# Output projection by block products: which weight parts are prepared in the attention, by which engine, and which in the stage itself

## The chip, the cores and the metric

One core of one Trainium2 chip runs the whole kernel. The metric is the device time of one execution in microseconds. Five engines work side by side, each in its own order of instructions: TensorE (PE in the profile; PEld is its weight load), VectorE (DVE), ScalarE (ACT), GpSimd (POOL) and SyncE (SP, which issues most DMAs).

## The reference

A decoder trunk of two layers, T = 1024 tokens, width D = 1024, all in fp32. Cut to the output projection and what stands on either side of it:

```python
merged = g_a * (o_a @ w_br[l, :OUT_A]) + g_b * (o_b @ w_br[l, OUT_A:])
x = x + merged @ w_o[l]                  # (1024, 1024) @ (1024, 1024)
h2 = rmsnorm(x, norm2[l])
up = h2 @ w_up[l]                        # then a ConvFFN, w_up is (1024, 5632)
```

Ahead of it stand an RMSNorm, one input projection, a dilated window attention (o_a) and a stick-breaking attention (o_b). g_a and g_b are sigmoids of gate columns of the input projection.

## The kernel before, in words

**Products.** Each fp32 operand x is kept as two parts in a reduced type, hi = round(x) and lo = x − hi; a product is three matmuls, hi·hi, hi·lo and lo·hi (`product`, L185). The parts come from `split` (L145): ACT casts hi (L148), DVE subtracts to lo (L156). Weights are loaded raw by SP into the tag "wr" (NRAW = 2 buffers) and split from there (`weights`, L164).

**The output projection** `merged @ w_o` takes w_o and the merged activations as 2 × 2 blocks and forms seven block products (k = 0 to 6) instead of eight, of sums and differences of blocks. Each product is four e-blocks of 128 output columns, and each e-block 12 matmuls: four i, three matmuls each. The order is 0, 4, 1, 2, 3, 5, 6 (`out_proj`, L1379). Four of the seven weight operands are sums or differences of blocks of w_o. After an e-block DVE adds the result to the residual x (L1455), and `norm_add` (L481) squares x on ACT (L487) and adds to a running sum of squares on DVE (L489). Sums for half 0 of x are done by k = 3, and PE takes them with a small product, nrm_t (L544), ahead of the second norm. Half 1 follows at the end of the stage.

**The weight operands are prepared ahead**, in the attention. `prepare` (L1328) is a generator: the scheduler of dense work (`share`, L312) asks it for one step per unit of dense work from the 15th on (PREP = 14). It takes four blocks of w_br and eight of w_o. A block is loaded into the tag "ot", which has one buffer (w_one); three steps later its parts follow, one a step. Each part, w_two, is an ACT copy (L1337), a DVE subtraction (L1338) and a DMA (L1339) to DRAM: `brd` for the branch weights, `wod` for the seven operands. Block sums are formed in place on DVE (L1342). That is 4 × 7 + 8 × 10 = 108 steps in a layer.

**The attention around it.** PE interleaves dense pairs of the input projection with attention items. The last pair is a values' pair (`pair_v`, L1294). For each of its quarters PE transposes into v_t (L1300), ACT and DVE make vv (L1305, L1306), and a DMA sends it off (L1311); vv too lives in "ot". Stick-breaking items (`stick_item`, L712) have scores z, a gate beta on ACT (L729), a diagonal select on GpSimd (L735), a scan and a product on DVE (L749, L756), transposes sb_t on PE, and outputs sb_o (L668) that DVE gathers in ob (L678).

**The branch stage** (in `mixer`, L1462) multiplies the two attention outputs by w_br (br_ps, L190 to L192), two outputs of columns to one loaded block br_w (`branch_in`, L1562), weighs with the gates (gin, L1620, L1625), merges, and forms sums c11, c12, c21 for the projection.

**The up projection.** `up_plain` (L1777) starts the first ffn unit: up_weights(0, 0) and (0, 1) are loaded and split (w_raw, w_hi, w_lo) when it starts, right behind the last block product; PE's u_ps (L190 to L192) uses them, and then takes nrm_t of half 1.

PE's instruction order comes from these generators. The scheduler places what ACT, DVE, GpSimd and SP do by priority; each engine then works strictly through its list.

Of the kernel before, what the change touches and what calls it, by code (L numbers as in the profile page):

```python
# [16 lines left out]
P = 128  # L17
# [48 lines left out]
def trunk_kernel(ctx, tc, x, norm1, w_in, b_gate, w_br, w_o, norm2, w_up, conv_w, conv_b, w_down, norm_f, out, depth=None, probe=None):  # L66
# [54 lines left out]
    wod = dr.tile([7, 4, P, 2, 512], F32, name="wod")  # L121
    brd = dr.tile([4, P, 2, T], F32, name="brd")
# [1205 lines left out]
    def prepare(l):  # L1328


        many = 0

        def out(src, there):
            nonlocal many
            t = small("w_two", F32R) if many % 2 else sb.tile([P, 512], F32R, tag="bias", name="w_two")
            many += 1
            act.copy(t[:, 0:256], src)  # L1337
            yields(dve.tensor_tensor(t[:, 256:512], src, f32(t[:, 0:256]), ALU.subtract))  # L1338
            nc.sync.dma_start(there, f32(t).rearrange("p (h n) -> p h n", h=2))  # L1339

        def into(dst, a, b, op):
            yields(dve.tensor_tensor(dst, a, b, op))  # L1342

        def load(src):
            raw = sb.tile([P, 4, 256], F32, tag="ot", name="w_one")
            nc.sync.dma_start(raw, src)
            return [raw[:, i, :] for i in range(4)]

        for e2 in range(4):
            blocks = load(w_br[l].rearrange("(k p) n -> p k n", p=P)[:, :, 256 * e2 : 256 * e2 + 256])  # L1350
            for _ in range(3):
                yield
            for k, x in enumerate(blocks):
                out(x, brd[e2][:, :, 256 * k : 256 * k + 256])
                yield
        for i in range(4):
            for c in range(2):
                raw = sb.tile([P, 2, 2, 256], F32, tag="ot", name="w_one")
                for j in range(2):
# [3 lines left out]
                for _ in range(3):  # L1363
                    yield
                col = slice(256 * c, 256 * c + 256)
                for k, x in ((0, a11), (3, a22), (4, a12)):
                    out(x, wod[k, i][:, :, col])
                    yield
                for k, dst, x, y, op in (
                    (2, a11, a11, a21, ALU.subtract),  # L1370
                    (5, a21, a21, a22, ALU.add),
                    (1, a22, a22, a11, ALU.subtract),
                    (6, a12, a12, a22, ALU.subtract),
                ):
                    into(dst, x, y, op)
                    out(dst, wod[k, i][:, :, col])
                    yield

    def out_proj(keep):  # L1379
# [7 lines left out]
        def load(at):  # L1387
            if at >= len(order):
                return
            k = order[at]  # L1390
            ws[k] = []
            for i in range(4):
                if at % 2 == 0:
                    if i % 2 == 0:
                        t = sb.tile([P, 2, 2, 512], F32R, tag="ql", bufs=2, name="wo_in")
                    nc.sync.dma_start(f32(t[:, i % 2]), wod[k, i])
                    ws[k].append((t[:, i % 2, 0, :], t[:, i % 2, 1, :]))
                else:
                    w = [sb.tile([P, 512], F32R, tag=tag, bufs=4, name="wo_in") for tag in ("wh", "wl")]
                    for h in range(2):  # L1400
                        nc.sync.dma_start(f32(w[h]), wod[k, i][:, h, :])
                    ws[k].append(w)
# [9 lines left out]

        def beside(k, e):
            c11, c12, c21 = keep[0, 0], keep[1, 0], keep[0, 1]
            if k == 0:
# [3 lines left out]
                split(*sums[1][e], c11[:, e, :])  # L1419
            elif k == 4:  # L1420
                dve.tensor_tensor(c21[:, e, :], c21[:, e, :], c11[:, e, :], ALU.subtract)
                if e == 0:
                    new_sum(2)
                split(*sums[2][e], c12[:, e, :])
                if e == 3:
                    x_in(1, 0)
            elif k == 1:
                if e == 0:
                    new_sum(3)
                split(*sums[3][e], c21[:, e, :])  # L1430
                if e == 3:
                    x_in(1, 1)
                    x_in(0, 1)

        load(0)
        load(1)
        yield
        for at, k in enumerate(order):
# [4 lines left out]
            for e in range(4):  # L1443
# [13 lines left out]
                if k > 2:  # L1457
                    norm_add(n, 4 * f + e, e == 0 and k in (4, 5), acc[:, n, :])
                yield
            load(at + 2)  # L1460

    def mixer(l, pending):  # L1462
# [140 lines left out]
        for i, ab in order:  # L1603
# [28 lines left out]
            if i == 9:  # L1632
                wo = out_proj(keep)
                next(wo)
# [16 lines left out]
    def ffn(l, pending, final):  # L1651
# [125 lines left out]
        def up_plain(j, order, turns, extra):  # L1777
# [3 lines left out]
            w = [up_weights(j, 0), up_weights(j, 1)]  # L1781
# [597 lines left out]
```

## Time and profile before

| | |
|---|---|
| median of 3 runs | 2703.09 us (2701.85 to 2704.11) |
| the profiled execution | 2700.12 us, span 2698.4 us, mean granted TensorE clock 0.984 |
| busy, share of the span | PE 96%, PEld 80%, DVE 80%, ACT 50%, POOL 4% |
| POOL | 111.4 us in 137 instructions |

How to read it: busy times are sums over one execution. A row of a timeline gives the start, the length, engine, line, operation, output <- inputs, and in brackets how long the engine had been idle and what ended that. `x4` is the number of equal instructions in a row. A releaser such as `DVE ob L678` is the last thing waited for by the profile. PEclk, or the column after the engines in a table of stretches, is the TensorE clock granted in that stretch, 1.00 being full. A matmul of 128 × 512 follows the one before by 0.23 us at full clock.

### The profile page before, as it was taken

Reading aid. Unit: us, or ns where it says so; the run is one execution under the profiler, and the core shown is the slowest. Engines: PE = TensorE matmul, PEld = TensorE weight load, DVE = VectorE, ACT = ScalarE, POOL = GpSimd, SP = SyncE. Lnnn points to the kernel's source line nnn. Section 1 sums busy time; section 2 is a strip of 40 time slices with the busy share of each in tenths; the row PEclk is TensorE's granted clock in tenths of the full one; section 3 lists DMA queues with packets and bytes.
Section 4 is the critical chain, followed back from the end, with each engine's and each line's share of the span. In section 5 each row is a group of like instructions: output and inputs, shape, how many; then the busy total and the mean of one; then the engine's idle time right before and its main releaser. Section 6 shows DMA issues by size and latency. Waiting matters only on the chain. (4 is left out here: it accounts for less than half of the span.)

```text
span 2698.4 us, 36486 instructions
## 1 busy us (share of the span) xinstructions
PE 2602.4 (96%) x12551; PEld 2164.6 (80%) x12551; DVE 2150.6 (80%) x3701; ACT 1361.9 (50%) x2609; POOL 111.4 (4%) x137
## 2 busy tenths in 40 slices
PE   9997899999899999999999978999998999999999
PEld 8876688887788888888887757888787888888887
DVE  8887777786788888897678878777858888888965
ACT  6555566663455555522445545665624545454224
POOL 3000000011000000000000020000200000000000
PEclk9998999999999999999999989999999999999999
DMA  7665667985234444588347656879752343546963
GB/s 251 217 225 189 203 192 211 253 280 217 76 130 159 152 145 159 210 334 319 142 154 230 220 173 201 220 203 259 271 203 71 136 158 137 172 141 247 340 249 127
DMA packets 428165, 537.75 MB, mean 199 GB/s; under 512 B 27700, under 2 KB 331468, under 8 KB 425164
## 3 DMA queue, kind: packets, MB, share of 16 engines
q1 hardware_dynamic: 427116, 533.02, 60.0%
q0 software_dynamic: 704, 2.13, 0.3%
q8 instruction: 99, 1.62, 0.2%
q14 instruction: 86, 0.70, 0.1%
q10 hardware_dynamic: 160, 0.27, 0.0%
HBM read 334.95 MB, written 200.38 MB: 198 GB/s over the span
## 5 line engine op out<-in xcount | busy, mean ns | idle before, releaser
L148 ACT CAST w_hi<-up_a 128x512 fp32r<-128x512 f32 x280 | 174.1, 623 | 277.3 <-DVE up_a L1827 120.3
L156 DVE TENSOR_TENSOR w_lo<-up_a,w_hi 128x512 fp32r<-128x512 f32 x280 | 189.4, 688 | 83.8 <-ACT w_hi L148 83.8
L148 ACT CAST w_hi<-in_a 128x512 fp32r<-128x512 f32 x252 | 155.9, 623 | 130.5 <-DVE in_a L1195 31.7
L156 DVE TENSOR_TENSOR w_lo<-in_a,w_hi 128x512 fp32r<-128x512 f32 x252 | 172.1, 686 | 60.3 <-ACT w_hi L148 57.2
L1984 DVE TENSOR_TENSOR x<-x,d_ps 128x512 f32<-128x512 f32 x220 | 150.2, 684 | 60.0 <-PE d_ps L1975 56.7
L1064 PE MATMUL u_a<-hh,w_hi 128*128 128x512 f32 x320 | 124.5, 389 | 0.0
L1065 PE MATMUL u_a<-hl,w_hi 128*128 128x512 f32 x320 | 124.5, 389 | 0.0
L1066 PE MATMUL u_a<-hh,w_lo 128*128 128x512 f32 x320 | 124.5, 389 | 0.0
L1064 PE MATMUL u_a<-t_hi,w_hi 128*128 128x512 f32 x320 | 124.5, 389 | 0.0
L1065 PE MATMUL u_a<-t_lo,w_hi 128*128 128x512 f32 x320 | 124.5, 389 | 0.0
L1066 PE MATMUL u_a<-t_hi,w_lo 128*128 128x512 f32 x320 | 124.5, 389 | 0.0
L1973 PE MATMUL d_ps<-gd_in,w_hi 128*128 128x512 f32 x316 | 123.2, 390 | 0.0
L1974 PE MATMUL d_ps<-gd_in,w_hi 128*128 128x512 f32 x316 | 123.0, 389 | 0.0
L1975 PE MATMUL d_ps<-gd_in,w_lo 128*128 128x512 f32 x316 | 122.9, 389 | 0.0
L1064 PE MATMUL i_a<-hh,w_hi 128*128 128x512 f32 x288 | 119.6, 415 | 0.1
L1064 PE MATMUL i_a<-t_hi,w_hi 128*128 128x512 f32 x288 | 117.2, 407 | 1.8 <-ACT u L1212 1.8
L1066 PE MATMUL i_a<-hh,w_lo 128*128 128x512 f32 x288 | 114.6, 398 | 0.0
L1065 PE MATMUL i_a<-hl,w_hi 128*128 128x512 f32 x288 | 114.0, 396 | 0.0
L1337 ACT CAST w_two<-w_one 128x256 fp32r<-128x256 f32 x144 | 57.5, 410 | 111.0 <-DVE w_one L1342 43.8
L1066 PE MATMUL i_a<-t_hi,w_lo 128*128 128x512 f32 x288 | 113.2, 393 | 0.0
L1065 PE MATMUL i_a<-t_lo,w_hi 128*128 128x512 f32 x288 | 113.1, 393 | 0.0
L1973 PE MATMUL d_ps<-gd_in,wd 128*128 128x512 f32 x284 | 111.0, 391 | 0.0
(423 smaller groups left out, 7895.2 us busy)
## 6 DMA issues: line engine op xcount, KB each, us to landing
gd<-g SPq DMA_DIRECT2D x154, 512.0 KB, 3.2
gd_in<-gd SPq DMA_DIRECT2D x154, 512.0 KB, 6.5
up_a<-in_w_up_dram SPq DMA_DIRECT2D x80, 512.0 KB, 5.1
in_a<-in_w_in_dram SPq DMA_DIRECT2D x72, 512.0 KB, 5.9
wod<-w_two SPq DMA_DIRECT2D x112, 256.0 KB, 2.5
wd_raw<-in_w_down_dram SPq DMA_DIRECT2D x22, 1024.0 KB, 13.1
wo_in<-wod SPq DMA_DIRECT2D x32, 512.0 KB, 4.9
gin<-gs SPq DMA_DIRECT2D x32, 512.0 KB, 4.8
```

The costliest lines, as they stand in the source:

```text
L148: one = act.copy(hi, src)
L156: two = dve.tensor_tensor(lo, src, f32(hi), ALU.subtract)
L1064: pe.matmul(o, w[0][:, c], rh, start=(first and i == 0), stop=False, skip_group_check=True)
L1065: pe.matmul(o, w[0][:, c], rl, start=False, stop=False, skip_group_check=True)
L1066: pe.matmul(o, w[1][:, c], rh, start=False, stop=(last and i == 3), skip_group_check=True)
L1337: act.copy(t[:, 0:256], src)
L1973: pe.matmul(o, wh[:, c], gh, start=(i == 0 and k in (0, 4, 5)), stop=False, skip_group_check=True)
L1974: pe.matmul(o, wh[:, c], gl, start=False, stop=False, skip_group_check=True)
L1975: pe.matmul(o, wl[:, c], gh, start=False, stop=(i == m - 1), skip_group_check=True)
L1984: dve.tensor_tensor(x, x, o, ALU.add)
```

## The change

`prepare` no longer makes parts of w_br, and takes seven steps for a w_o block, 56 in a layer. It makes the parts of k = 0, 4, 2 and 1 alone, with the subtraction on GpSimd; the block sums too move to GpSimd, and the two of k = 5 and 6 go to DRAM unsplit (`wof`). So a layer has 32 ACT copies here instead of 72, 64 GpSimd operations, and none on DVE.

`out_proj` loads k = 0, 4, 1 and 2 ready, in halves; k = 3 raw from w_o, k = 5 and 6 raw from `wof`, through "wr" (`load_raw`), and splits them on ACT and DVE in the stage (`two`). Squares of x are added one product earlier or later by a rule of their own (`square`), and the residual half x_in(1, 1) is fetched earlier. The first up weights are loaded and split beside k = 5 (`early["up"]`). `branch_in` loads raw w_br (half the bytes) through "wr" and splits it.

```diff
 def out(src, there):
     act.copy(t[:, 0:256], src)
-    yields(dve.tensor_tensor(t[:, 256:512], src, f32(t[:, 0:256]), ALU.subtract))
+    pool.tensor_tensor(t[:, 256:512], src, f32(t[:, 0:256]), ALU.subtract)
     nc.sync.dma_start(there, f32(t).rearrange("p (h n) -> p h n", h=2))
...
-for e2 in range(4):
-    blocks = load(w_br[l].rearrange("(k p) n -> p k n", p=P)[:, :, 256 * e2 : 256 * e2 + 256])
-    for _ in range(3):
-        yield
-    for k, x in enumerate(blocks):
-        out(x, brd[e2][:, :, 256 * k : 256 * k + 256])
-        yield
...
-for k, x in ((0, a11), (3, a22), (4, a12)):
-    out(x, wod[k, i][:, :, col])
-    yield
-for k, dst, x, y, op in (
-    (2, a11, a11, a21, ALU.subtract),
-    (5, a21, a21, a22, ALU.add),
-    (1, a22, a22, a11, ALU.subtract),
-    (6, a12, a12, a22, ALU.subtract),
-):
-    into(dst, x, y, op)
-    out(dst, wod[k, i][:, :, col])
-    yield
+out(a11, wod[0, i][:, :, col])
+yield
+out(a12, wod[4, i][:, :, col])
+pool.tensor_tensor(a11, a11, a21, ALU.subtract)
+yield
+out(a11, wod[2, i][:, :, col])
+pool.tensor_tensor(a21, a21, a22, ALU.add)
+nc.sync.dma_start(wof[0, i][:, col], a21)
+yield
+pool.tensor_tensor(a22, a22, a11, ALU.subtract)
+out(a22, wod[1, i][:, :, col])
+pool.tensor_tensor(a12, a12, a22, ALU.subtract)
+nc.sync.dma_start(wof[1, i][:, col], a12)
+yield
...
+def load_raw(k):
+    raws[k] = []
+    for i in range(0, 4, 2):
+        t = sb.tile([P, 2, 512], F32, tag="wr", bufs=NRAW, name="wo_raw")
...
+        nc.sync.dma_start(t, src)
+        raws[k] += [t[:, 0, :], t[:, 1, :]]
+def two(k, *some):
...
+    for i in some:
+        split(*ws[k][i], raws[k][i])
...
+elif k == 2:
+    square(0, 0, e, True)
+    if e in (1, 2):
+        two(3, 2 * e - 2, 2 * e - 1)
+    if e == 2:
+        load_raw(5)
+elif k == 3:
+    square(0, 1, e, False)
+    if e < 2:
+        two(5, 2 * e, 2 * e + 1)
+    if e == 1:
+        load_raw(6)
+    if e == 3:
+        two(6, 0, 1, 2, 3)
+elif k == 5:
+    square(1, 1, e, True)
+    if e == 0:
+        early["up"] = []
+    if e < 2:
+        early["up"].append(weights(w_up[l][:, e * DFF : e * DFF + P], P))
+else:
+    square(1, 0, e, False)
...
 e, wb = todo[i][1], big("br_w", F32R)
-nc.sync.dma_start(f32(wb), brd[e // 2])
+raw = sb.tile([P, 4, 256], F32, tag="wr", bufs=NRAW, name="br_raw")
+nc.sync.dma_start(raw, w_br[l].rearrange("(k p) n -> p k n", p=P)[:, :, e * P : (e + 2) * P])
+for q in (1, 0):
+    split(*parts_[q], raw[:, 2 * q : 2 * q + 2, :])
...
-w = [up_weights(j, 0), up_weights(j, 1)]
+w = early.pop('up') if j == 0 else [up_weights(j, 0), up_weights(j, 1)]
```

**What it moves.** PE's order is the same before and after. At three places the order of other engines differs; the numbers in a name only tell one buffer's use from another.

The first place is ACT at the last values' pair of the attention, layer 0. Before, parts of a w_o block (w_two) and the splits of dense inputs (in_a) and scores (sb_t) come ahead of three vv in a row:

```order
L1337 CAST w_two_2908<-w_one_2770 128x256
L1337 CAST w_two_2923<-w_one_2770 128x256
L148 CAST sbh_2932<-sb_t_2927 128x512
L148 CAST w_hi_2937<-in_a_2592 128x512
L1337 CAST w_two_2957<-w_one_2770 128x256
L1337 CAST w_two_2973<-w_one_2770 128x256
L1305 CAST vv_2809<-v_t_2804 128x4x2x64
L1305 CAST vv_2873<-v_t_2868 128x4x2x64
L1305 CAST vv_2952<-v_t_2947 128x4x2x64
L148 CAST w_hi_2988<-in_a_2592 128x512
```

After, at the same place:

```order
L1305 CAST vv_2759<-v_t_2754 128x4x2x64
L148 CAST sbh_2774<-sb_t_2770 128x384
L677 COPY fold_2796<-sb_o_2648 64x256
L148 CAST w_hi_2781<-in_a_2577 128x512
L1251 COPY last_2808<-i_a_2587 128x512
L1305 CAST vv_2815<-v_t_2810 128x4x2x64
L729 ACTIVATE beta_2819<-z_2820 128x512
L730 ACTIVATE stay_2735<-z_2820 128x512
L148 CAST w_hi_2831<-in_a_2577 128x512
L1212 COPY u_2835<-i_a_2838 128x512
```

No w_two is left there; the first vv stands ahead of `last`, and each of the next is further along, with work of the pair between them.

The second place is GpSimd in the stick-breaking items of layer 0. Before, it does selects only:

```order
L689 MEMSET slots_898 64x4x256
L735 AFFINE_SELECT beta_1019<-beta_1019 128x128
L735 AFFINE_SELECT beta_1044<-beta_1044 128x128
L735 AFFINE_SELECT beta_1075<-beta_1075 128x128
L735 AFFINE_SELECT beta_1160<-beta_1160 128x128
L735 AFFINE_SELECT beta_1310<-beta_1310 128x128
```

After, from the same clearing of `slots` on (L1338 makes a part, L1355 to L1363 form the block sums):

```order
L689 MEMSET slots_898 64x4x256
L1338 TENSOR_TENSOR w_two_1240<-w_one_1193,w_two_1240 128x256
L1355 TENSOR_TENSOR w_one_1193<-w_one_1193 128x256
L1358 TENSOR_TENSOR w_one_1193<-w_one_1193 128x256
L1361 TENSOR_TENSOR w_one_1193<-w_one_1193 128x256
L735 AFFINE_SELECT beta_1019<-beta_1019 128x128
L735 AFFINE_SELECT beta_1044<-beta_1044 128x128
L1338 TENSOR_TENSOR w_two_1284<-w_one_1193,w_two_1284 128x256
L735 AFFINE_SELECT beta_1075<-beta_1075 128x128
L735 AFFINE_SELECT beta_1160<-beta_1160 128x128
L1338 TENSOR_TENSOR w_two_1259<-w_one_1193,w_two_1259 128x256
```

The same selects, 1019, 1044 and 1075, stand behind and between parts and block sums of the first w_o block.

The third place is DVE at the end of the output stage, layer 0. Before, the up weights' parts w_lo come after the last sum of squares (L489):

```order
L156 TENSOR_TENSOR t_lo_7237<-s3_7252,t_hi_7236 128x512
L156 TENSOR_TENSOR t_lo_7237<-s3_7262,t_hi_7236 128x512
L489 TENSOR_TENSOR nrm_6560<-nrm_6560,sq_7273 128x512
L156 TENSOR_TENSOR t_lo_7237<-s3_7276,t_hi_7236 128x512
L489 TENSOR_TENSOR nrm_6560<-nrm_6560,sq_7293 128x512
L156 TENSOR_TENSOR w_lo_7299<-w_raw_7296,w_hi_7298 128x512
L156 TENSOR_TENSOR w_lo_7305<-w_raw_7302,w_hi_7304 128x512
L156 TENSOR_TENSOR w_lo_7311<-w_raw_7308,w_hi_7310 128x512
L156 TENSOR_TENSOR w_lo_7317<-w_raw_7314,w_hi_7316 128x512
L547 RECIPROCAL ss_7334<-ss_7334 128x4
```

After, they stand at product k = 3, between the adds to x0 (L1490, before L1455) and the sums of squares of half 0:

```order
L489 TENSOR_TENSOR nrm_6428<-nrm_6428,sq_6920 128x512
L156 TENSOR_TENSOR w_lo_7016<-w_raw_7013,w_hi_7015 128x512
L1490 TENSOR_TENSOR x0_6829<-x0_6829,o_ps_6594 128x512
L156 TENSOR_TENSOR w_lo_7022<-w_raw_7019,w_hi_7021 128x512
L489 TENSOR_TENSOR nrm_6428<-nrm_6428,sq_6942 128x512
L1490 TENSOR_TENSOR x0_6829<-x0_6829,o_ps_6595 128x512
L156 TENSOR_TENSOR w_lo_7052<-w_raw_7049,w_hi_7051 128x512
L489 TENSOR_TENSOR nrm_6428<-nrm_6428,sq_6966 128x512
L156 TENSOR_TENSOR w_lo_7058<-w_raw_7055,w_hi_7057 128x512
L1490 TENSOR_TENSOR x0_6829<-x0_6829,o_ps_6596 128x512
L489 TENSOR_TENSOR nrm_6428<-nrm_6428,sq_6982 128x512
```

And the end of the stage now reads:

```order
L156 TENSOR_TENSOR t_lo_7151<-s3_7166,t_hi_7150 128x512
L156 TENSOR_TENSOR t_lo_7151<-s3_7176,t_hi_7150 128x512
L489 TENSOR_TENSOR nrm_6428<-nrm_6428,sq_7187 128x512
L156 TENSOR_TENSOR t_lo_7151<-s3_7190,t_hi_7150 128x512
L489 TENSOR_TENSOR nrm_6428<-nrm_6428,sq_7207 128x512
L547 RECIPROCAL ss_7224<-ss_7224 128x4
```

The four w_lo have moved from behind the last sum of half 1 to ahead of the last sum of half 0; the order of what ends the stage is otherwise the same.

More of the change, by code (lines that the diff above doesn't have):

```diff
@@ L120, in trunk_kernel @@
     gd = dr.tile([NF // 2, 7, P, 2, HF], F32, name="gd")
-    wod = dr.tile([7, 4, P, 2, 512], F32, name="wod")
-    brd = dr.tile([4, P, 2, T], F32, name="brd")
+    wod = dr.tile([5, 4, P, 2, 512], F32, name="wod")
+    wof = dr.tile([2, 4, P, 512], F32, name="wof")
     obd = dr.tile([P, 2, T], F32, name="obd")
@@ L1411, in part, with square @@
             return h_part(int(k > 4), 2 * i + int(k in (4, 6)))
+        def square(n, f, e, first):
+            norm_add(n, 4 * f + e, first and e == 0, acc[:, n, :])
         def beside(k, e):
@@ L1419, in beside @@
                 split(*sums[1][e], c11[:, e, :])
+                if e == 3:
+                    load(1)
             elif k == 4:
-                dve.tensor_tensor(c21[:, e, :], c21[:, e, :], c11[:, e, :], ALU.subtract)
                 if e == 0:
```

58 lines of the change are left out of this document (29 added, 29 removed).

## The prediction

> **What bounds the kernel now.** I read the engines' shares first, then the list of what TensorE waits for, then a table of the stretches in which its clock was low, and last the rows around each long wait. The first part of the page:
>
> ```profile
> PE 2602.4 (96%) x12551; PEld 2164.6 (80%) x12551; DVE 2150.6 (80%) x3701; ACT 1361.9 (50%) x2609; POOL 111.4 (4%) x137
> ```
>
> TensorE is the bound: 2602 us of a span of 2698.4. The change leaves its matmuls and their order as they are, so it can only win what TensorE loses in waits, and in the slow clock behind them. The list of waits, TensorE only, both layers together (total, times, longest):
>
> ```profile
> PE u_ps L192 <- DVE w_lo L156: 15.1, 2, 7.5
> PE v_t L1300 <- DVE vv L1306: 13.2, 2, 6.7
> PE v_t L1300 <- DVE ob L678: 9.7, 2, 5.1
> PE br_ps L190 <- DMA br_w<-brd: 9.0, 3, 4.3
> PE sb_o L668 <- DVE ob L678: 8.5, 2, 4.5
> PE sb_o L668 <- DVE vv L1306: 6.7, 2, 3.3
> ```
>
> Three families stand out. Four rows (v_t and sb_o) belong to the last values' pair of the attention, 250 to 310 us in layer 0 and 1585 to 1645 in layer 1: 13.2 + 9.7 + 8.5 + 6.7 = 38.1 us. One (br_w) is the branch products' weights, 9.0 us. One (u_ps) is the first up product behind the output projection, 15.1 us. Each is followed by a stretch at half clock. The table of stretches (length, TensorE's busy time and matmuls, weight loads, DVE, ACT, POOL, then the granted clock):
>
> ```profile
> 252.47:259.30 6.83, 4.73 (x13) 3.89 (x14) 5.48 (x11) 4.05 (x9) 0.56 (x1) 0.50 0.30 94
> 266.13:276.37 10.24, 4.11 (x14) 3.25 (x15) 2.33 (x5) 1.70 (x4) 0.00 (x0) 0.50 0.46 166
> 303.67:307.09 3.42, 2.90 (x9) 2.48 (x10) 2.51 (x5) 0.37 (x1) 0.00 (x0) 0.50 0.85 268
> 610.87:617.70 6.83, 4.81 (x11) 3.80 (x12) 6.66 (x10) 4.62 (x9) 2.57 (x2) 0.50 0.78 244
> 706.45:716.68 10.23, 4.87 (x13) 3.91 (x14) 6.33 (x11) 3.30 (x6) 0.00 (x0) 0.50 0.18 53
> 1587.08:1590.50 3.42, 3.39 (x10) 2.90 (x11) 3.16 (x6) 2.33 (x5) 0.56 (x1) 0.50 0.36 115
> 1597.32:1610.98 13.66, 6.52 (x21) 5.25 (x22) 4.37 (x9) 4.05 (x8) 0.00 (x0) 0.50 0.40 144
> 1638.28:1641.70 3.42, 3.42 (x10) 2.65 (x9) 1.55 (x3) 1.62 (x4) 0.29 (x1) 0.50 0.63 217
> ```
>
> At clock 0.50 half of the busy time is loss. For the values' pair that is (4.73 + 4.11 + 2.90 + 3.39 + 6.52 + 3.42) / 2 = 12.5 us, so the whole family costs 38.1 + 12.5 = **50.6 us**. The br_w family costs 9.0 + 4.81 (half of it, in two layers) = 13.8, the u_ps family 15.1 + 4.87 = 20.0. All three: 84.4.
>
> **The values' pair: +50.6.** Timeline rows of TensorE and ACT there, in layer 0, then two groups with their durations (least, median, most, in ns) and the start of their first and last:
>
> ```profile
> 254.57 1.12 PE L1300 MATMUL v_t<-ident,u 128*128 128x128 f32 x4 [5.14 <-DVE ob L678]
> 268.92 1.11 PE L1300 MATMUL v_t<-ident,u 128*128 128x128 f32 x4 [6.44 <-DVE vv L1306]
> ```
> ```profile
> 252.82 0.40 ACT L1337 CAST w_two<-w_one 128x256 fp32r<-128x256 f32 x1 [4.11 <-DMA w_one<-in_w_o_dram]
> ```
> ```profile
> 266.65 0.40 ACT L1337 CAST w_two<-w_one 128x256 fp32r<-128x256 f32 x1 [0.40 <-DMA wod<-w_two]
> 267.55 0.59 ACT L1305 CAST vv<-v_t 128x512 fp32r<-128x512 f32 x1 [0.49 <-DVE w_two L1338]
> 271.92 0.59 ACT L1305 CAST vv<-v_t 128x512 fp32r<-128x512 f32 x1 [3.79 <-DMA sv<-vv]
> ```
> ```profile
> L1300 PE MATMUL v_t<-ident,u x72: 270/272/476, 243.9 to 1770.1; 128*128 128x128 f32 x72
> ```
> ```profile
> L1337 ACT CAST w_two<-w_one x144: 399/407/467, 76.9 to 1662.2; 128x256 fp32r<-128x256 f32 x144
> ```
>
> ACT stands 4.11 us at a weight part whose load has not landed. DVE's subtraction of that part stands behind it, and ob (L678), which needs nothing of the weights, is queued next on DVE; TensorE waits for ob until 254.57. Then vv and w_one take turns in the one buffer "ot". All parts of the block come first, the last at 266.65, and three vv come in a row from 267.55, 4.4 us apart because each waits for the DMA of the one before. TensorE meets them at 268.92 (6.44) and once more. The wait near 304 is again ob behind a part.
>
> In the changed order there are 56 steps of preparation instead of 108, paced by the same clock. The part at 266.65 is step 88 (28 steps of branch parts, six blocks of 10), the first at 76.9 is step 4: 189.75 / 84 = 2.26 us a step. 56 steps end near 76.9 + 52 × 2.26 = 194, ahead of the pair's first v_t at 243.9. No w_one is left in "ot" then, each vv follows its v_t, and ob has no part ahead of it. What is late next? The two v_t rows lie 14.35 us apart; without the 6.44 and half of the 4.73 it is 5.5, more than the 4.4 that one vv takes. So the chain keeps up by a microsecond, and I leave nothing of the wait.
>
> **The preparation on GpSimd: −4 (−20 to +10).** The nearest rows for what is taken away and what it is put on:
>
> ```profile
> L1338 DVE TENSOR_TENSOR w_two<-w_one,w_two 128x256 fp32r<-128x256 f32 x144 | 59.2, 418 | 49.2 <-ACT w_two L1337 46.5 <-DMA slots<-sq 1.2 <-DMA obd<-ob 0.5
> ```
> ```profile
> L735 POOL TENSOR_SCALAR_AFFINE_SELECT beta<-beta 128x128 f32<-128x128 f32 x64 | 44.7, 700 | 593.8 <-ACT beta L729 530.6 <-DVE w_lo L156 30.9 <-DVE w_one L1342 25.2
> L1585 POOL TENSOR_TENSOR hl<-m_part,hh 128x512 fp32r<-128x512 f32 x16 | 24.7, 1550 | 161.2 <-ACT hh L1584 161.2
> L2270 POOL TENSOR_TENSOR h_raw<-hh,hl 128x256 f32<-128x256 f32 x8 | 7.1, 914 | 0.0
> ```
>
> Per layer DVE loses 72 parts of 0.42 us and 32 block sums of the same shape (43.5 us), ACT 40 of its 72 parts of 0.41; GpSimd gains 64. No row has this shape as a subtraction on GpSimd beside a busy DVE. From below 0.91 us (L2270, same size, nothing beside it), from above 1.55 (L1585, twice the size, DVE full). I take 0.95, nearest to the row of the same size: 64 × 0.95 = 61 us in some 120. That fits, so the preparation does end before the pair. The price is that the 15 or so diagonal selects per layer (L735), now run at once, stand behind up to five or six parts in GpSimd's queue; behind the select stand DVE's L756 on the same scores and TensorE's transposes. TensorE has other work there, so most of it is hidden; I take 2 us a layer. Ends: 10 lost a layer (every select 0.7 us late on the path), or 5 gained (DVE freed of what it did for the preparation until 194: half of the 43.5).
>
> The Trainium skill, "GPSIMD Engine Reference", section 3.1, speaks against this part: two-input elementwise work takes twice as long there as on VectorE, so VectorE should keep it. The rows agree on the ratio (0.914 to 0.42 us); by the rule the step would lose, but GpSimd is 4% busy here and DVE 80%, and I side with those shares; what is left of the rule is rival D.
>
> **The branch stage: 0 (−8 to +8).** brd is gone, raw branch weights are split in the stage. Rows of TensorE and of DVE, the second from just ahead of TensorE's wait:
>
> ```profile
> 612.89 0.77 PE L190 MATMUL br_ps<-oh_a,br_w 128*128 128x512 f32 x1 [4.34 <-DMA br_w<-brd]
> ```
> ```profile
> 607.88 0.68 DVE L1620 TENSOR_TENSOR gin<-gin,br_ps 128x512 f32<-128x512 f32 x1
> ```
>
> The wait named is the DMA's, from 608.5 to 612.89. But by the program's order this L1620 takes the 20th product, and TensorE has finished 24: DVE is four behind and works on without a gap until 625. The changed order has one more DVE operation up to the last gate (four splits of br_w in, three c21 and one m_lo out: 64 for 63). Removing the DMA's wait moves the wait to DVE, and TensorE's 4.3 us stay under another name. Ends: the DMA wait goes (+4 a layer), or a second split late behind the gates costs as much.
>
> **The output stage: −6 (−20 to 0).** The k = 3, 5 and 6 weights come raw, through the two "wr" buffers, then the up weights through the same two.
>
> ```profile
> 682.16 0.69 DVE L489 TENSOR_TENSOR nrm<-nrm,sq 128x512 f32<-128x512 f32 x1 [0.76 <-ACT sq L487]
> ```
> ```profile
> 683.24 0.95 PE L544 MATMUL nrm_t<-ones,nrm 128*128 128x1 f32 x8
> ```
> ```profile
> wo_in<-wod SPq DMA_DIRECT2D x32, 512.0 KB, 4.9
> ```
>
> The first half's sum of squares is done at 682.85 and TensorE takes it at 683.24 with no slack. In the changed order this last add on DVE stands behind the fourth up split. One block of a product is 12 matmuls of 0.22 us (0.44 at half clock, from the rows of the next part), a product four blocks, 10.6 us. The row at 683.24 stands one block behind the end of k = 3, so k = 3 begins near 683.2 − 2.6 − 10.6 = 670; raw6 is asked for at its second block, about 674, lands 4.9 later at 679, is split by 681, and only then is its buffer free for the second up part: landed at 684 to 686, cast, split and add 2 us more. I take 3 us late a layer, from 0 (the loads overlap better) to 7, or 10 with the clock. That the clock falls after a short wait is seen here:
>
> ```profile
> 179.30 0.50 PE L1064 MATMUL i_c<-hh,w_hi 128*128 128x512 f32 x1 [2.19 <-ACT u L1217]
> ```
> ```profile
> 180.79:184.21 3.42, 3.42 (x12) 2.83 (x11) 3.13 (x6) 1.89 (x5) 0.42 (x1) 0.50 0.50 130
> ```
>
> After 2.19 us of idling came 3.42 us at half clock, 1.7 us lost. The Trainium skill, "TensorE: Matmul & The Clock Gate", section "HAM oscillation", has as its rule that gaps over about 3.4 us are the ones to avoid. By that rule a new 3 us wait would cost no clock, and this part's low end would be −14; this trace says that it may, and it decides.
>
> **The first up product: +6 (4 to 10), not 20.** Rows at the end of the stage:
>
> ```profile
> 710.47 0.68 DVE L489 TENSOR_TENSOR nrm<-nrm,sq 128x512 f32<-128x512 f32 x1
> 711.07 1.28 DVE L156 TENSOR_TENSOR w_lo<-w_raw,w_hi 128x512 fp32r<-128x512 f32 x2
> ```
> ```profile
> 703.87 0.39 PE L191 MATMUL u_ps<-hl,w_hi 128*128 128x512 f32 x1
> 711.81 0.80 PE L192 MATMUL u_ps<-hh,w_lo 128*128 128x512 f32 x1 [7.55 <-DVE w_lo L156]
> ```
> ```profile
> 716.24 1.16 PE L544 MATMUL nrm_t<-ones,nrm 128*128 128x1 f32 x8
> ```
>
> From 711.81 TensorE does 10 matmuls in 4.43 us at half clock, 0.44 each. With w_lo early it does them right behind the one at 703.87, at 0.22 each, until 706.3, and then needs the second half's sum of squares. DVE ends that at 711.15, and its queue up to there is the same and without gaps. So a wait of 4.7 takes the place of 7.55: nrm_t comes 5 us sooner, less 2 us of half clock that then falls on later matmuls. 3 a layer.
>
> **Sum.** 50.6 − 4 + 0 − 6 + 6 = 46.6. The profiled execution took 2700.12 (1.7 around its span), 2.97 less than the median: 2700.1 − 46.6 + 3.0 = **2656**.
>
> **Rivals.** (B) All three families go: −84, **2619**. For it: each has its cause removed by name. Against: the add at 710.47, and DVE four products behind at 607.88. (C) The stage's new chain through "wr" is slow, TensorE waits 10 us or more a layer at nrm_t with the clock halved, and something of the values' pair stays: half the gain, **2678**. (D, slower) The selects behind the parts on GpSimd hold DVE and then TensorE. With 30 selects it eats all 46.6 from 1.6 us each on; at 3 us each, which six parts in a row at L1585's 1.55 would give (up to 9 us for one), it is 2703.1 + 90 − 46.6 = **2746**. Against it: parts of 0.9 us, and TensorE's spare work. (E) The change doesn't do what it says: at over 2.9 us a part (64 × 2.9 = 186 us) GpSimd is still preparing at 260, the vv wait in "ot" as now, and it comes out near **2702**.
>
> **Numbers.** A measurement here tells about 0.2% (5.4 us) from no change. Forecast 0.63, C 0.19, B 0.09, D 0.06, E 0.03. Faster 0.91, same 0.03, slower 0.06. The range takes in the forecast's own spread (all terms at a bad end don't come together) and C to 2688; at the other end it takes 26 us more than forecast, 2630. B, D and E are left out, 0.18.
>
> **What would show it.** Right: no w_two on ACT after about 200 us; v_t and sb_o gone from TensorE's waits; full clock from 250 to 310; a br_ps wait on DVE or gates; nrm_t waiting on nrm (L489) in place of u_ps on w_lo. Wrong: waits of sb_t or z that rise before 215 (D); parts on GpSimd well over 1 us; a wait of nrm_t near 683 over 5 us (C); no wait near 706 (B).

## The result, and the profile after

The changed kernel took 2670.71 us (median of 4 runs, 2669.2 to 2671.88), the kernel before beside it 2702.47. The ratio is 0.9882, with a 95% interval of 0.9865 to 0.9899: faster by 31.8 us, where 46.6 had been forecast. Its profiled execution took 2670.32 us, its span is 2668.6.

The engines' shares in the changed kernel:

```profile
PE 2597.4 (97%) x12551; PEld 2163.0 (81%) x12551; DVE 2137.4 (80%) x3533; ACT 1358.8 (51%) x2569; POOL 226.0 (8%) x265
```

TensorE is where it was; GpSimd has doubled, from 111.4 to 226.0 us. The list of TensorE's waits, after (total, times, longest):

```profile
PE i_a L1064 <- DVE u L1242: 13.1, 4, 5.5
PE nrm_t L544 <- DVE nrm L489: 12.3, 5, 4.8
PE i_b L1064 <- DVE u L1228: 10.2, 6, 2.3
PE br_ps L192 <- DVE br_w L156: 5.1, 3, 2.2
PE z L654 <- ACT stay L730: 4.6, 6, 2.6
PE i_c L1064 <- ACT u L1217: 4.3, 2, 2.2
PE i_c L1064 <- ACT last L1251: 3.7, 4, 1.3
```

All four rows of the values' pair are gone, as is u_ps on w_lo; nrm_t on nrm stands in its place, as forecast. Two more rows are new, i_a and i_b on u, 23.3 us together. They belong to the dense pairs of the attention, and their places say where. The same two stretches of layer 0, first of the kernel before, then of the changed one (length, busy time and instructions of PE, PEld, DVE, ACT, POOL, then the granted clock and the DMA columns):

```profile
76.00:216.00 140.00, 133.43 (x654) 108.67 (x652) 114.94 (x207) 78.32 (x177) 6.73 (x16) 0.99 0.68 220
216.00:340.00 124.00, 100.27 (x466) 80.50 (x467) 97.37 (x180) 67.18 (x148) 7.96 (x13) 0.90 0.58 190
```
```profile
76.00:216.00 140.00, 117.56 (x557) 93.86 (x556) 102.98 (x137) 67.97 (x152) 67.69 (x79) 0.97 0.61 199
216.00:340.00 124.00, 123.53 (x629) 102.53 (x628) 100.30 (x160) 70.08 (x142) 10.61 (x17) 0.99 0.44 143
```

After 216 us TensorE is now busy nearly without a break, 123.5 of 124 us at clock 0.99. But from 76 to 216, where it had been nearly as full (133.4 of 140), it is down to 117.6. That is the stretch in which GpSimd works 67.7 us.

TensorE's instructions have the same order in both kernels, so their starts can be set side by side, one by one. In layer 0 the changed kernel is 0.96 us ahead near 27 us and 21.1 behind at 204 (times of before): **22.0 lost**. It is 13.1 ahead at 355: **34.1 won**. In layer 1 it loses 21.7 and wins 34.2. The branch stage wins 2.6 and 4.3; from the first block product into the up projection it is 0.9 slower in layer 0 and 1.1 faster in layer 1. Together 68.3 − 43.7 + 6.9 + 0.2 = 31.7. That this is nearly the gain of the medians, 31.8, is chance: the two executions set side by side differ by 29.8 in span. Beside the terms of the sum stand 1.0 us won ahead of 27 us and 2.3 lost between the attentions and the branch stages (1.6 and 0.8).

So what is to be explained above all is one number: 22 us a layer lost before 205 us, where the prediction had 2. Rows of the largest wait there (ACT, DVE and TensorE of the changed kernel):

```profile
206.31 0.41 ACT L1337 CAST w_two<-w_one 128x256 fp32r<-128x256 f32 x1 [7.46 <-DMA w_one<-in_w_o_dram]
206.62 0.58 ACT L148 CAST sbh<-sb_t 128x512 fp32r<-128x512 f32 x1
```
```profile
207.29 0.69 DVE L156 TENSOR_TENSOR sbl<-sb_t,sbh 128x512 fp32r<-128x512 f32 x1 [5.51 <-ACT sbh L148]
207.90 0.98 DVE L1192 TENSOR_TENSOR in_a<-in_a 128x512 f32<-128x512 f32 x1
210.97 1.23 DVE L156 TENSOR_TENSOR w_lo<-in_a,w_hi 128x512 fp32r<-128x512 f32 x1 [2.10 <-ACT w_hi L148]
212.12 0.67 DVE L1242 TENSOR_TENSOR u<-u,i_b 128x512 f32<-128x512 f32 x1
```
```profile
212.94 0.77 PE L1064 MATMUL i_a<-hh,w_hi 128*128 128x512 f32 x1 [5.51 <-DVE u L1242]
```

They offer two readings. ACT stands 7.46 us at a part whose block has not landed, with the cast sbh behind it, DVE behind that, and TensorE at the end: the stall of the values' pair over again, in another place. Or one looks at the lengths: w_lo takes 1.23 us in place of 0.68, L1192 takes 0.98.

**Theory 1, the one buffer**: the reload of w_one waits for GpSimd's last block sum and for the DMA that sends the sum off, and ACT waits for the reload. **Theory 2, GpSimd beside DVE**: GpSimd's work makes DVE's operations longer, and DVE is what TensorE waits for here.

### The profile page after: what moved, and what is told of

Read it like the earlier page. It is cut to its first block, busy times and chain, and to the rows that moved or that the text cites. A ratio compares the mean times of both kernels' runs of the same rounds, so it can differ in the third digit from the quotient of the medians.

```text
span 2668.6 us, 36222 instructions
## 1 busy us (share of the span) xinstructions
PE 2597.4 (97%) x12551; PEld 2163.0 (81%) x12551; DVE 2137.4 (80%) x3533; ACT 1358.8 (51%) x2569; POOL 226.0 (8%) x265
## 4 chain that ended last, share of the span: by engine, by line
PE 67%; DVE 4%; DMA 3%; ACT 2%; issue 1%; POOL 1%; SPq 1%; DVEq 0%; POOLq 0%; ACTq 0%
PE u_a L1066 5%; PE u_a L1064 5%; PE u_a L1065 5%; PE d_ps L2008 5%; PE d_ps L2010 5%; PE d_ps L2009 5%; PE u_c L1064 3%; PE u_c L1066 3%; PE u_c L1065 3%; PE i_a L1064 2%; PE i_a L1065 2%; PE i_a L1066 2%; PE u_b L1066 1%; PE u_b L1064 1%; PE u_b L1065 1%
## 5 line engine op out<-in xcount | busy, mean ns | idle before, releaser
L156 DVE TENSOR_TENSOR w_lo<-in_a,w_hi 128x512 fp32r<-128x512 f32 x252 | 183.5, 731 | 74.0 <-ACT w_hi L148 68.1
L148 ACT CAST w_hi<-in_a 128x512 fp32r<-128x512 f32 x252 | 155.8, 621 | 148.2 <-DVE in_a L1195 32.5
L1064 PE MATMUL i_a<-hh,w_hi 128*128 128x512 f32 x288 | 120.2, 417 | 13.4 <-DVE u L1242 13.1
L2008 PE MATMUL d_ps<-gd_in,wd 128*128 128x512 f32 x284 | 111.1, 391 | 0.0
L2010 PE MATMUL d_ps<-gd_in,wd 128*128 128x512 f32 x284 | 110.5, 389 | 0.0
```

Source lines behind the costliest of these rows:

```text
L148: one = act.copy(hi, src)
L156: two = dve.tensor_tensor(lo, src, f32(hi), ALU.subtract)
L1064: pe.matmul(o, w[0][:, c], rh, start=(first and i == 0), stop=False, skip_group_check=True)
L2008: pe.matmul(o, wh[:, c], gh, start=(i == 0 and k in (0, 4, 5)), stop=False, skip_group_check=True)
L2010: pe.matmul(o, wl[:, c], gh, start=False, stop=(i == m - 1), skip_group_check=True)
```

## The experiments

**Five steps of lead.** The first part of a block comes two steps later.

```diff
-                yield
-                yield
-                yield
+                for _ in range(5):
+                    yield
```

> The changed kernel with two more steps between the load of a w_o block and its first part (five instead of three), so 72 steps in a layer. What is to be explained: against the kernel before, the changed one loses some 22 us a layer in the attention between 27 and 205 us. Theory 1, the one buffer: w_one is reloaded into a single buffer, the next load waits for GpSimd's last block sum and the DMA that sends it off, and ACT stands at the first part until the load has landed (53.8 us in both layers), with casts for the dense pair behind it and DVE and TensorE behind those. It expects ACT's wait at w_two for w_one's DMA to fall below 20 us, TensorE's waits i_a and i_b on u to fall by more than half, and 2645 us (2636 to 2655). Theory 2, GpSimd beside DVE: 61 us of GpSimd work a layer makes DVE's operations longer (w_lo 0.87 in place of 0.68 us) and holds selects and parts; the spacing changes nothing of that. It expects 2671 us, give or take 4.

Measured: 2666.25 us (2662.87 to 2668.48). Theory 1's range is missed by 11 us, and Theory 2's (2667 to 2675) by 0.8 us. One sign of Theory 1 did come: TensorE's waits of i_a and i_b on DVE's u fell from 23.3 us to 6.1. But others took their place, z on stay with 17.8 us (4.6 in the changed kernel) and i_a on ACT's u (L1221) with 7.9. And the edit did not do what it was for: ACT's wait for w_one only went from 53.8 us to 49.1, fewer and longer (13 in place of 19). So this run decides little between the two.

**The preparation on DVE.** All 64 GpSimd operations a layer go back.

```diff
-            pool.tensor_tensor(t[:, 256:512], src, f32(t[:, 0:256]), ALU.subtract)
+            yields(dve.tensor_tensor(t[:, 256:512], src, f32(t[:, 0:256]), ALU.subtract))
...
-                pool.tensor_tensor(a11, a11, a21, ALU.subtract)
+                yields(dve.tensor_tensor(a11, a11, a21, ALU.subtract))
```

(and the other three sums likewise)

> The changed kernel with the parts' subtractions and the block sums of the preparation back on DVE (64 operations of 0.42 us a layer), everything else as changed. Theory 2, GpSimd beside DVE, expects most of the 22 us a layer back: 2640 us (2630 to 2650), and DVE's w_lo at 0.68 us. Theory 1, the one buffer, expects a part of it, since a block is done some 2 us sooner and its buffer is free sooner, while DVE is fuller: 2662 us (2655 to 2672), with ACT's wait at w_two for w_one's DMA still over 35 us.

Measured: 2636.92 us (2633.57 to 2638.92), ratio to before 0.975 (0.9736 to 0.9765). Theory 2's number; **GpSimd costs 33.8 us in this change** (35.7 by the two ratios to the kernel before). The group of the dense pairs' w_lo, two inputs in on-chip memory, and that of sbl, whose sb_t comes from TensorE's accumulators, from 76 to 216 us: first the changed kernel, then this one.

```profile
L156 DVE TENSOR_TENSOR w_lo<-in_a,w_hi 128x512 fp32r<-128x512 f32 x31 | 26.7, 866 | 8.7 <-ACT w_hi L148 8.3
L1199 DVE TENSOR_TENSOR in_a<-in_a 128x512 f32<-128x512 f32 x10 | 9.2, 918 | 0.2
L156 DVE TENSOR_TENSOR sbl<-sb_t,sbh 128x512 fp32r<-128x512 f32 x11 | 7.5, 684 | 10.1 <-ACT sbh L148 7.5 <-DMA wod<-w_two 2.7
L1242 DVE TENSOR_TENSOR u<-u,i_b 128x512 f32<-128x512 f32 x5 | 3.4, 671 | 0.0
```
```profile
L156 DVE TENSOR_TENSOR w_lo<-in_a,w_hi 128x512 fp32r<-128x512 f32 x37 | 24.9, 682 | 4.8 <-ACT w_hi L148 4.4
L1199 DVE TENSOR_TENSOR in_a<-in_a 128x512 f32<-128x512 f32 x10 | 6.9, 694 | 0.0
L156 DVE TENSOR_TENSOR sbl<-sb_t,sbh 128x512 fp32r<-128x512 f32 x12 | 8.2, 684 | 1.2 <-ACT sbh L148 1.1
L1242 DVE TENSOR_TENSOR u<-u,i_b 128x512 f32<-128x512 f32 x5 | 3.4, 680 | 0.0
```

w_lo is back from 866 to 682 ns and L1199 from 918 to 694. Those with an input from the accumulators, sbl and L1242, never changed. And ACT still waits 32.3 us for w_one here, while TensorE loses only 3 to 4 us a layer in the stretch that cost 22: Theory 1's wait is real and mostly hidden.

**Both edits.**

> Both edits: five steps of lead and the preparation on DVE. Theory 1, the one buffer, expects about the time of the five steps alone, 2645 us (2636 to 2655). Theory 2, GpSimd beside DVE, expects the time of the preparation on DVE alone, 2640 us (2630 to 2650). If each carries half, this is faster than either alone by 8 us or more.

Measured: 2633.65 us, ratio 0.9743 (0.9728 to 0.9757). This is the preparation on DVE alone, within their intervals; the lead adds nothing that can be told.

**Half of the GpSimd work, either half.** First the sums stay on GpSimd and the parts go to DVE, then the other way about.

```diff
-            pool.tensor_tensor(t[:, 256:512], src, f32(t[:, 0:256]), ALU.subtract)
+            yields(dve.tensor_tensor(t[:, 256:512], src, f32(t[:, 0:256]), ALU.subtract))
```

> The changed kernel with only the block sums (32 a layer) on GpSimd, the parts' subtractions back on DVE. With all 64 on GpSimd it took 2670.7, with none 2636.9. Two ways in which GpSimd can cost these 34 us. Theory 2a, length: while GpSimd reads the same memory DVE's operations take longer, whoever waits for the result; half the operations cost half, 2654 us (2648 to 2660). Theory 2b, chain: ACT's copies of the sums, the DMAs of the raw sums and the reload of w_one hang on four sums in a row on GpSimd; nearly all of the cost stays, 2666 us (2660 to 2672).

Measured: 2654.79 us (2653.11 to 2655.85).

```diff
-                pool.tensor_tensor(a11, a11, a21, ALU.subtract)
+                yields(dve.tensor_tensor(a11, a11, a21, ALU.subtract))
```

(and the other three sums likewise)

> The other half: the parts' subtractions (32 a layer) on GpSimd, the block sums on DVE. Theory 2a, length, expects half the cost again, 2654 us (2648 to 2660). Theory 2b, chain: nothing but a DMA hangs on the parts, and next to nothing is lost, 2640 us (2634 to 2646).

Measured: 2653.41 us (2651.85 to 2654.89). Half the operations cost half, whichever half. But this does not part length from waiting yet. It had been expected that only a DMA hangs on the parts; in the second run DVE also waits for them, since a block sum overwrites what the part before it reads:

```profile
DVE w_one L1355 <- POOL w_two L1338: 25.3, 10, 5.4
```

In the first, ACT waits 15.0 us for GpSimd's sums.

**GpSimd work that nobody reads.** The preparation on DVE, and beside each part five subtractions into a scratch tile; a later run has three.

```diff
+            for j in range(5):
+                pool.tensor_tensor(scratch, f32(t[:, 32 * j : 32 * j + 96]), f32(t[:, 32 * j + 32 : 32 * j + 128]), ALU.subtract)
             nc.sync.dma_start(there, f32(t).rearrange("p (h n) -> p h n", h=2))
```

> The preparation on DVE (as in the run that took 2636.9), and beside each part five added subtractions of 128x96 on GpSimd, into a scratch tile that nobody reads: 160 a layer, some 60 us of GpSimd work like the changed kernel's. Only the part's buffer is held a little longer, and selects stand behind them as before. Theory 2a, length, expects most of the 34 us: 2665 us (2655 to 2675), w_lo in the attention well over 0.75 us. Theory 2b, chain, expects little: 2640 us (2634 to 2648).

Measured with five: 2669.43 us (2666.86 to 2671.51), 32.5 above the run without them.

```profile
L1342 POOL TENSOR_TENSOR scratch<-w_two 128x96 f32<-128x96 f32 x320 | 182.1, 569 | 145.1 <-ACT w_two L1339 122.5
```
```profile
L156 DVE TENSOR_TENSOR w_lo<-in_a,w_hi 128x512 fp32r<-128x512 f32 x31 | 23.1, 754 | 1.3 <-ACT w_hi L148 1.1
L756 DVE TENSOR_TENSOR beta<-beta,stay 128x512 f32<-128x512 f32 x8 | 5.4, 695 | 6.2 <-POOL beta L735 6.1
```

A loss as large as the change's is there though nobody reads what the added operations make. It took more GpSimd time, though (182 us against 123 in the changed kernel), and there are waits of another kind: in the second row DVE's product stands 6.1 us behind selects that stand behind the added work, and ACT waits 16.5 us in all (L1339) for part buffers that the added work still reads.

> As the run with five added subtractions beside each part (2669.4; they took 182 us of GpSimd in both layers, against 123 us for the changed kernel's preparation), but with three: 192 in all, some 109 us. If the cost goes with the time in which GpSimd reads beside DVE (theory 2a, length), it is three fifths of the 32.5 us: 2636.9 + 19.5 = 2656 us (2650 to 2663). If it is a queue of five in a row that holds the selects, three cost far less than that: 2643 us (2637 to 2649).

Measured with three: 2653.02 us (2651.64 to 2654.44), 16.1 above the run without them: in the range of length (2650 to 2663) and outside that of a queue (2637 to 2649), though three fifths of the added operations cost half of the 32.5.

**One input in place of two.**

```diff
-                pool.tensor_tensor(scratch, f32(t[:, 32 * j : 32 * j + 96]), f32(t[:, 32 * j + 32 : 32 * j + 128]), ALU.subtract)
+                pool.tensor_copy(scratch, f32(t[:, 32 * j : 32 * j + 96]))
```

> Five added operations beside each part as in the run that took 2669.4, but copies with one input in place of subtractions with two, of the same 128x96. If DVE is slowed by whatever GpSimd does in that memory, the cost goes with GpSimd's time in them: some 0.18 us for each us of it, over 12 us in all, 2650 us or more. If it takes two inputs to hold DVE up, DVE's operations stay at their length (w_lo 0.68) and the time at 2637 to 2641 us.

Measured: 2647.41 us (2644.05 to 2651.6), between the two expectations.

```profile
L1342 POOL COPY scratch<-w_two 128x96 f32<-128x96 f32 x320 | 148.7, 465 | 154.5 <-ACT w_two L1339 136.6
```
```profile
L156 DVE TENSOR_TENSOR w_lo<-in_a,w_hi 128x512 fp32r<-128x512 f32 x35 | 24.3, 702 | 1.0 <-ACT w_hi L148 0.7
L756 DVE TENSOR_TENSOR beta<-beta,stay 128x512 f32<-128x512 f32 x8 | 5.3, 688 | 4.1 <-POOL beta L735 4.0
```

Copies lengthen DVE's operations little (w_lo 702), while the selects still come late (4.0). By the table below 5.5 of the 10.5 us that they cost can be length; that the late selects are the rest was not tried apart, and ACT waits for GpSimd here too (17.7 us).

All these runs can be put into one table. For each the DVE operations of both attentions (70 to 250 and 1390 to 1570 us) were taken one by one, and what each took over the median of the same operation, output and shape in the run with the preparation on DVE was added up:

| | GpSimd busy there | DVE lengthened by | time over 2636.9 | the same by the ratios |
|---|---|---|---|---|
| sums on GpSimd | 82.9 | 18.6 | 17.9 | 18.1 |
| parts on GpSimd | 78.4 | 13.9 | 16.5 | 17.3 |
| both (the change) | 146.8 | 33.2 | 33.8 | 35.7 |
| three subtractions beside | 134.2 | 19.1 | 16.1 | 13.8 |
| five subtractions beside | 202.6 | 30.0 | 32.5 | 33.2 |
| five copies beside | 165.8 | 5.5 | 10.5 | 8.4 |

The last column is there because the kernel before, run again beside each group of runs, came out between 2702.5 and 2707.7 us in the median: it is the difference of the ratios times 2702.8. Over the five rows with subtractions the time lost follows what DVE is lengthened by, within 3 us (within 6 by the ratios), and not GpSimd's own busy time.

Two of the rows also answer the rival that waiting for GpSimd is the price. With three subtractions DVE waits 2.0 us for GpSimd and ACT 15.2, with five copies 10.1 and 17.7; yet the subtractions, with less waiting, cost more, 16.1 to 10.5, and they are what lengthens DVE (19.1 to 5.5). The lengthening can be seen in single operations too. In the changed kernel the 34 w_lo that run while GpSimd subtracts take 1.00 us in the mean, the 191 beside which GpSimd is idle 0.69; of the sbl 6 run beside a subtraction and 40 beside nothing, and both kinds take 0.68 to 0.69.

Theory 2 holds. That the two sums are equal is a finding of these runs; step by step it was not traced, and where GpSimd's operations stand five in a row the late selects may carry some of it.

**The up weights late.** The early load was taken out:

```diff
-                if e == 0:
-                    early["up"] = []
-                if e < 2:
-                    early["up"].append(weights(w_up[l][:, e * DFF : e * DFF + P], P))
...
-            w = early.pop('up') if j == 0 else [up_weights(j, 0), up_weights(j, 1)]
+            w = [up_weights(j, 0), up_weights(j, 1)]
```

> The changed kernel with the first up weights loaded and split at the start of the first ffn unit again, not beside k = 5. The prediction's terms: the early load costs a wait ahead of the first nrm_t (1.48 and 1.04 us in the changed kernel) and saves 5 us a layer at the first up product less 2 us of clock. So it expects TensorE's wait of 7.5 us at u_ps for w_lo back, the wait at the first nrm_t gone, and 2674 us (2670 to 2680). Rival: the early load is worth the whole wait of 7.5 us and its clock, 10 us a layer, 2690 us. A second rival: it is worth nothing, 2671 us, since the sum of squares ends last either way.

Measured: 2670.97 us (2666.92 to 2677.23), no change. But the order of instructions was no other: w_lo stands among the sums of half 0 as before the edit, since the scheduler moves the load up once wh and wl are free, and what frees them is that k = 5 no longer lies there. So k = 5 was put back as well:

```diff
-            if k in (5, 6):
+            if k == 6:
...
-            elif k in (4, 2):
+            elif k in (4, 2, 5):
```

> The changed kernel with the up weights really late. In the run without the early load the order of instructions had w_lo in the same early place (the scheduler moves it up as soon as its buffers wh and wl are free, and k = 5 no longer takes them), so that run told nothing. Here k = 5 is kept in wh and wl, as before the change, and the load stands in the first ffn unit; w_lo is behind the last sum of squares again. The prediction's terms are 3 us a layer lost at the first nrm_t and 3 won at the first up product; by the changed kernel's own rows 1.3 us of idling there are given back and a wait of 7.5 in place of 4.8 is taken. So 2674 us (2671 to 2678), with u_ps waiting 7.5 us for w_lo twice. Rival, the early load is worth the whole wait with its clock, 10 us a layer: 2690 us.

Measured: 2672.92 us (2671.79 to 2678.42). TensorE's wait for w_lo is back:

```profile
PE u_ps L192 <- DVE w_lo L156: 15.1, 2, 7.5
```

Taking away this 15.1 us wait was worth nothing that can be told: 2.2 us by the times, and the other way by the ratios (0.9879 here, 0.9882 for the changed kernel). That fits the prediction's two terms (3 lost, 3 won a layer), and rules out the rival of 10 us a layer (2690 us).

**The branch weights alone.** The kernel before, without branch parts in the preparation and with the raw load in the stage; all seven operands of w_o are still prepared, 80 steps on ACT and DVE.

```diff
-        for e2 in range(4):
-            blocks = load(w_br[l].rearrange("(k p) n -> p k n", p=P)[:, :, 256 * e2 : 256 * e2 + 256])
...
-                nc.sync.dma_start(f32(wb), brd[e // 2])
+                raw = sb.tile([P, 4, 256], F32, tag="wr", bufs=NRAW, name="br_raw")
...
+                for q in (1, 0):
+                    split(*parts_[q], raw[:, 2 * q : 2 * q + 2, :])
```

> The kernel before with one part of the change: the branch weights are not prepared but loaded raw and split in the branch stage. All seven operands of w_o are prepared as before, on ACT and DVE, 80 steps in a layer, and the up weights come as before. 80 steps at 2.26 us from 76.9 end near 249 us, about where the values' pair begins. If ending before the pair is what counts, nearly all of its 50 us go and the branch stage gains 3 us a layer: 2650 us (2643 to 2662). Rival: the last block still stands among the first vv and ob, half of the waits stay: 2675 us (2665 to 2685).

Measured: 2660.98 us (2658.69 to 2662.6), ratio 0.9842 (0.9827 to 0.9856). One part of the change, alone, gives more than the change as a whole. No v_t or ob row is left among its waits; TensorE's largest are u_ps (15.1) and i_c on u (14.4). Splitting k = 3, 5 and 6 in the stage as well is worth the rest to 2636.9, some 24 us, with what comes along.

**The version that the runs point to.** The preparation on DVE, the early load kept, k = 5 in wh and wl, so that w_lo comes behind the first half's sum.

> The version that the runs point to: preparation on DVE (2636.9 alone), the up weights still loaded beside k = 5, but k = 5 kept in wh and wl, so that w_lo comes behind the first half's last sum of squares and ahead of the second's. The waits ahead of the first nrm_t (1.5 and 1.0 us in the changed kernel) should go: 2634 us (2630 to 2638). Rival: w_lo then waits for k = 5's last matmul and comes among the second half's sums, which end last, 1 to 3 us a layer later: 2640 us.

Measured: 2633.69 us (2631.67 to 2636.44), ratio 0.9727 (0.971 to 0.9745): 1.6% under the changed kernel's ratio of 0.9882. Its intervals overlap with those of the two other versions on DVE, and its longest wait at nrm_t is now 7.1 us, so that the room given to w_lo is no shown gain.

## Why the prediction was right, and where not

**The values' pair: right.** 25.3 us a layer were forecast for its waits and their clock. Set side by side, TensorE wins 25.9 us in layer 0 (229.5 to 305 us of before) and 26.7 in layer 1 (1567 to 1642). The reason holds too: the branch part alone, 80 steps, already empties these rows. The preparation ended at 217 us in layer 0 and not near 194, which is still ahead of the pair's first v_t.

**What else waits in that stretch: left out.** Around the pair (204 to 229.5 and 305 to 355 us of before, and the same places in layer 1) another 8.2 and 7.6 us were won. The prediction has no term for them; its list of waits passes over these rows of the kernel before:

```profile
PE i_c L1064 <- ACT u L1217: 7.2, 4, 2.2
PE z L654 <- ACT stay L730: 6.7, 6, 2.7
```

The small waits that the kernel before has in these stretches, of z, i_c, sb_t and sb_o, come to 5.3 and 6.1 us; the rest was not traced. That hid a part of the error below.

**The preparation on GpSimd: this is the step that failed.** "I take 0.95" a part was right (60.2 + 17.8 + 16.4 + 15.3 + 13.0 = 122.7 us for 128 operations, 0.96). "That fits" was true as well: GpSimd had the time. But the price was put at 2 us a layer, for selects in GpSimd's queue, and the low end at 10; the runs on DVE put it at 17 a layer (33.8 / 2; another 3 to 4 of the 22 are lost there with DVE too). What was not priced at all is that DVE's own operations grow. The groups of the preparation in the changed kernel:

```profile
L1338 POOL TENSOR_TENSOR w_two<-w_one,w_two 128x256 fp32r<-128x256 f32 x64 | 60.2, 945 | 165.3 <-ACT w_two L1337 150.0 <-DMA kv<-sk 13.1 <-DMA w_one<-in_w_o_dram 2.2
...
L1361 POOL TENSOR_TENSOR w_one<-w_one 128x256 f32<-128x256 f32 x16 | 17.8, 1114 | 1.1
L1363 POOL TENSOR_TENSOR w_one<-w_one 128x256 f32<-128x256 f32 x16 | 16.4, 1023 | 1.3
L1358 POOL TENSOR_TENSOR w_one<-w_one 128x256 f32<-128x256 f32 x16 | 15.3, 957 | 4.8 <-DMA w_one<-in_w_o_dram 3.7
L1355 POOL TENSOR_TENSOR w_one<-w_one 128x256 f32<-128x256 f32 x16 | 13.0, 815 | 1.1
```

The profile of before had shown it: in its branch stage, where GpSimd does subtractions (L1585), this group of DVE has one shape and a mean well over the 0.68 us of its like. The 14 of them that run beside such a subtraction take 0.98 us in the mean, the 10 beside which GpSimd is idle 0.68:

```profile
L1625 DVE TENSOR_TENSOR m_part<-gin 128x512 f32<-128x512 f32 x24 | 20.6, 857 | 0.4
```

I also weighed the Trainium skill's rule against GpSimd for elementwise work ("GPSIMD Engine Reference", section 3.1) against the shares of busy time, and sided with the shares. The measured side is the rule's: the same change with DVE doing this work is 33.8 us faster, though DVE is the 80% engine. The reason that section gives is the longer time of one operation on GpSimd; the larger price here was what the work did to DVE's operations.

**The branch stage: nearly.** 0 was forecast, within −4 to +4 a layer; 2.6 and 4.3 were won. A wait on DVE took the DMA's place, as said, but a shorter one:

```profile
588.85 0.50 PE L192 MATMUL br_ps<-oh_a,br_w 128*128 128x512 f32 x1 [2.22 <-DVE br_w L156]
```

**The output stage and the first up product: right.** −6 and +6 were forecast, and the stage came out 0.9 slower in one layer and 1.1 faster in the other. Set side by side, 3.4 us were lost ahead of the first up product and 2.5 won at it in layer 0, 1.3 and 2.4 in layer 1, where 3 and 3 a layer had been taken. TensorE's rows at the two sums of squares of layer 0, after:

```profile
670.82 1.05 PE L544 MATMUL nrm_t<-ones,nrm 128*128 128x1 f32 x8 [1.48 <-DVE nrm L489]
```
```profile
700.62 1.84 PE L544 MATMUL nrm_t<-ones,nrm 128*128 128x1 f32 x8 [4.78 <-DVE nrm L489]
```

A wait of 4.7 was to take the place of 7.55; it is 4.78. The wait ahead of the first is 1.48 (and 1.04 in layer 1) in place of the 3 that I took. In the last run with the up weights late, where w_lo stays behind, the profile shows no such wait. That the order of w_lo moved because of the early load, as the section on the change has it, was wrong: the room in wh and wl moved it.

**The sum.** The forecast of 2656 was too low by 15 us; the measured time is inside the range. The early stretch came out 40 us below its term (−43.7 for −4), and 25 of these came back elsewhere: 16 in the small waits, 7 in the branch stage, 2 in the pair. That is luck: without these 25 us, for most of which the prediction has no term, the time would have been near 2695, outside its range. Of the rivals none came as described. C's time is near what was measured, but not by its mechanism: the wait ahead of the first nrm_t is 1.48 us and not 10, and nothing of the values' pair stays (and half of 46.6 would have put it at 2680, not 2678). D named the right engine, and one of its signs came faintly (a wait of 1.7 us at sb_t before 216 us in layer 0, where the kernel before shows none); but its mechanism, selects held in the queue, is the smaller one: DVE waits 5.5 us for them in the whole changed kernel, against 33.2 us by which its operations grew.

## What to carry to other kernels

An engine that is idle 96% of the time is not free: price what its work does to the operations of its neighbour, not only its own time and its queue, and look for a stage of the same profile where the two already run together. When a change has several parts, time them apart: here one part alone (2661.0) beat the whole (2670.7), and the whole without one bad part was better than both (2636.9). And when a load moves in the order, ask which buffer's release moved it before crediting the line that asks for it.

## What the runs showed of the hardware

A two-input subtraction on GpSimd lengthens DVE's two-input operations that run beside it when both inputs are in on-chip memory (w_lo from 0.68 to 0.87 us in the mean of a stretch, single ones to 1.23), and leaves those alone that read one input from the accumulators (sbl 0.684 both times, L1242 0.67). The preparation's GpSimd operations lengthened too: the 12 that ran while DVE was idle took 0.73 us in the mean, all 128 took 0.96. A one-input copy on GpSimd does far less: 148.7 us of copies lengthened DVE by 5.5 us, 182.1 us of subtractions by 30.0. The Trainium skill, "GPSIMD Engine Reference", section 1, says that the two share their way into this memory, with contention for DVE's instructions with two inputs there; these rows agree.
